# Hyena's short convolution: past tokens into the middle product, coming tokens into an array preloaded with the bias, joined later by VectorE

## The chip, the cores and the metric

The kernel runs on one core of one Trainium2 chip. The metric is device time in microseconds (us), from the start to the end of one execution; several runs are taken and their median counts. Beside these runs one execution was recorded by the hardware profiler; its trace gives every instruction's start and duration. Five engines work side by side, each through its own instruction stream in a fixed order: TensorE (PE in the profile; PEld is its weight load), VectorE (DVE), ScalarE (ACT), GpSimd (POOL) and SyncE (SP). In this kernel SP and POOL, and ACT for a few constants, issue the DMA transfers.

## The reference

One encoder layer on 256 tokens of width 2048, all in float32. A wide projection of the input feeds two branches, a chunked gated linear attention (GLA) and an order-2 Hyena; sigmoid gates mix the two, one output projection, a layer norm, a squared-ReLU MLP and a second layer norm follow. The change touches the Hyena branch alone:

```python
def _short_conv(u, w, b):                 # 3 taps along the tokens, per channel
    y = lax.conv_general_dilated(u, w[:, None, :], (1,), [(1, 1)], ...)
    return y + b
...
uc = _short_conv(u, conv_w, conv_b)
v, x1, x2 = jnp.split(uc, 3, axis=-1)
z = v
for o, gate in enumerate((x1, x2)):
    zf = jnp.fft.rfft(z, n=2 * L, axis=1)
    zc = jnp.fft.irfft(zf * filt_f[None, :, o], n=2 * L, axis=1)[:, :L]
    z = gate * (zc + skip[o] * z)
```

So each token's value is tap 0 times the token before it, plus tap 1 times itself, plus tap 2 times the token after it, plus a bias.

## The kernel before

**Stages.** The opening and the q, k, r projections with the Hyena filters (lines 251 to 505); v and the first gate with the GLA (511 to 691); the Hyena stage (694 to 827); the second gate's projection `g2` (841 to 845); the two branches' output projections and the merge; `w_out` and layer norm; the MLP. Weights come in blocks of 128 x 2048 (1 MB). Every float32 product is made of three: `split_hi_lo` (83) has ACT cast a block half to `whi` and DVE subtract to get `wlo`, and PE multiplies high by high, high by low and low by high.

**Weight stream.** `fetch` (92) issues the load of the block two ahead of the one in use, on SP, and its two splits. There are three raw buffers and three each of half-blocks `whi` and `wlo`, so a split of a half-block waits until PE has finished with the half-block three before it.

**A token group** (`token_group`, 208) makes one 256 x 512 piece of a projection: 4 blocks, 96 matmuls (lines 204 to 206), into two of the four banks of the PSUM pool `mmp`, one for each half of the tokens. After each block it calls `pump` (117), which counts a clock on by one and runs what `later(d, fn)` (113) has put off until then, in the order of due time and then of entry. So `later(3, ...)` entered at a group's end is run behind the third block of the next group.

**Order.** The program is traced in that order; a planner then fixes each engine's order. It takes, of the instructions whose inputs are there by its own estimate, the one traced first. `tc.keep_in_program_order` pins an instruction behind the one traced before it on its engine. On the chip every engine keeps the planned order and waits where an input is late, with all that stands behind it.

**Buffers.** A pool's tag with one buffer is used by one tile after the other: the first write of the next tile waits until the last instruction that uses the tile before is done, wherever that was traced. `qp` and `hp` have one buffer per tag. Tag `G` of `qp` (16 KB in a partition) holds `g_sb` (495), then `conv_sb` (699), then `g2_sb` (841).

**Hyena stage.** Four rounds `s`, each with the token groups `uv`, `ux`, `ux` (for v, x1, x2; 512 channels each) and a group `go` of the GLA's output projection. At the end of the first three stands `short_conv` (706). It makes three products of the group's PSUM banks with tap rows on DVE: `past` (tap 0), `y` (tap 1, the tile `cv` or `cx` in the profile) and `ahead` (tap 2), each in two halves (line 710, six instructions). It adds the bias to `y` (711). Then four POOL DMAs (718) add `past`, one partition on, and `ahead`, one partition back, into `y`, each with a 2 KB one for the row that goes over from one half of the tokens to the other. The `ahead` pair writes what the `past` pair wrote, so it waits for it to land. `conv_sb` has the tap rows and the bias row (1 MB, loaded anew for each group, line 704), `past` and `ahead`.

Behind each `uv` group 4 Hyena steps `j` are entered (2 chunks of 256 channels times 2 orders): `hy_load` (`Tl`, the filter's spectrum), `hy_fwd` (transform, 6 matmuls), `hy_mul` (DVE: `Z`, `pa`, `pb`, then the split `Yh`, `Yl`) and `hy_inv` (6 matmuls `yp`, the gate product `zf`, and for the second order a transpose `yT` of `zf` and its store `yo`, `yd`). Step j's `hy_fwd` and `hy_mul` are due 7 + 4j blocks behind the `uv` group and its `hy_inv` 11 + 4j, each time behind a third block. The last round's steps run on into the `g2` groups; the inverse of its last step is due behind the third block of the third of them.

Of the kernel before, what the change touches and what calls it, by code (L numbers as in the profile page):

```python
# [9 lines left out]
F32 = mybir.dt.float32  # L10
F32R = mybir.dt.float32r
I32 = mybir.dt.int32
AF = mybir.ActivationFunctionType
ALU = mybir.AluOpType
DRAM = bass.MemoryType.DRAM

P = 128
D = 2048
L = 256
NT = L // P  # L20
# [7 lines left out]
CW = D // NCH  # L28
# [14 lines left out]
def block_kernel(  # L43
# [24 lines left out]
    nc = tc.nc  # L68
    MM = nc.tensor.matmul

    base = ctx.enter_context(tc.tile_pool(name="base", bufs=1))
# [3 lines left out]
    drp = ctx.enter_context(tc.tile_pool(name="drp", bufs=1, space=DRAM))  # L75
# [4 lines left out]
    def psum_side(name):  # L80
        return sdp.tile([P, 512], F32, tag="sd", name=name)

    def split_hi_lo(hi, lo, src):
        return (nc.scalar.copy(hi, src),  # L84
                nc.vector.tensor_tensor(lo, src, hi.bitcast(F32), op=ALU.subtract))  # L85
# [20 lines left out]
    def weight_half(n, h):  # L106
        return (wp.tile([P, D // 2], F32R, tag="whi", bufs=3, name=f"whi{n}_{h}"),
                wp.tile([P, D // 2], F32R, tag="wlo", bufs=3, name=f"wlo{n}_{h}"))
# [4 lines left out]
    def later(d, fn):  # L113
        clock[1] += 1
        side.append((clock[0] + d, clock[1], fn))
# [92 lines left out]
    def token_group(act, name):  # L208
        pss = [psum_main(f"{name}_{tb}") for tb in range(NT)]
        for b in range(4):  # L210
            token_products(pss, act, [next_block()], range(NT), b)
            pump()
        return pss
# [34 lines left out]
    qp = qkg.enter_context(tc.tile_pool(name="qp", bufs=1))  # L248
# [5 lines left out]
    with tc.tile_pool(name="xp", bufs=1) as xp, tc.tile_pool(name="xq", bufs=1) as xq:  # L254
# [25 lines left out]
        for i in range(3):  # L280
            t = weight_half(-1, i)
# [52 lines left out]
    def mm3(ps, lh, ll, rh, rl, start, stop, hold=False):  # L334
        ins = MM(ps, lh, rl, start=start, stop=False)
        if hold:
            tc.keep_in_program_order(ins)
        MM(ps, lh, rh, start=False, stop=False)
        MM(ps, ll, rh, start=False, stop=stop)
# [130 lines left out]
    for i in range(2 * NCH):  # L470
        c, o = divmod(i, 2)
# [223 lines left out]
    hp = hstk.enter_context(tc.tile_pool(name="hp", bufs=1))  # L695
    cst = {}
    yh_dram = {}

    conv_sb = qp.tile([P, 4, 2 * 512], F32, tag="G", name="conv_sb")
    taps = conv_sb[:, 0:2].rearrange("p a b -> p (a b)").rearrange("p (a b) -> p a b", a=4)  # L700
    past, ahead = (conv_sb[:, 2 + i].rearrange("p (t d) -> p t d", t=NT) for i in range(2))

    def load_taps(i):
        nc.sync.dma_start(conv_sb[:, 0:2].rearrange("p a b -> p (a b)"), conv_rows[i:i + 1, :].broadcast_to([P, 2048]))

    def short_conv(pss, i, tag, name):
        y = hp.tile([P, NT, 512], F32, tag=tag, name=name)
        for j, dst in ((0, past), (1, y), (2, ahead)):
            for tb in range(NT):
                nc.vector.tensor_tensor(dst[:, tb], pss[tb], taps[:, j], op=ALU.mult)  # L710
        nc.vector.tensor_tensor(y, y, taps[:, 3:4].broadcast_to([P, NT, 512]), op=ALU.add)
        for dst, src in (
            (y[1:P], past[0:P - 1]),
            (y[0:1, 1], past[P - 1:P, 0]),
            (y[0:P - 1], ahead[1:P]),
            (y[P - 1:P, 0], ahead[0:1, 1]),
        ):
            nc.gpsimd.dma_start(dst, src, accum_op=ALU.add)
        if i + 1 < 12:
            later(2, lambda: load_taps(i + 1))  # L720
        return y

    def hy_v(s):
        def run():
            z = tuple(hp.tile([P, NT, 512], F32R, tag=t, name=f"{t}{s}") for t in ("vh", "vl"))
            split_hi_lo(z[0], z[1], cst.pop(("v", s)))
            for i in range(2):
                cst[("z", 2 * s + i, 0)] = tuple(t[:, :, i * CW:(i + 1) * CW] for t in z)
        return run

    def gate_part(n, c):
        return cst[(n, c // 2)][:, :, c % 2 * CW:(c % 2 + 1) * CW]

    def hy_load(c, o):
        def run():
            t = hp.tile([P, 2, 3, CW], F32, tag="Tl", name=f"Tl{c}{o}")
            nc.gpsimd.dma_start(t, T_dram[(c, o)])
            cst[("T", c, o)] = t
        return run

    def hy_fwd(c, o):
        def run():
            t = cst.pop(("T", c, o))
            zh, zl = cst.pop(("z", c, o))
            z = hp.tile([P, 3, 2, CW], F32, tag="Z", name=f"Z{c}{o}")
            for ri in range(2):
                pz = psum_side(f"Zp{c}{o}{ri}")
                mm3(pz.rearrange("p (a b) -> p a b", a=2), dfth[:, ri], dftl[:, ri], zh, zl, True, True, hold=True)
                nc.scalar.copy(z[:, 2:0:-1, ri, :], pz.rearrange("p (a b) -> p a b", a=2))
            cst[("Z", c, o)] = (t, z)  # L750
        return run

    def hy_mul(c, o):
        def run():
            t, z = cst.pop(("Z", c, o))
            a = hp.tile([P, 3, 2, CW], F32, tag="pa", name=f"pa{c}{o}")
            b = hp.tile([P, 3, 2, CW], F32, tag="pb", name=f"pb{c}{o}")
            TT = nc.vector.tensor_tensor
            full = [P, 3, 2, CW]
            TT(z[:, 0], z[:, 1], z[:, 2], op=ALU.add)  # L760
            TT(a, z, t[:, 0, :, None, :].broadcast_to(full), op=ALU.mult)
            TT(b, z[:, :, ::-1, :], t[:, 1, :, None, :].broadcast_to(full), op=ALU.mult)
            TT(a[:, :, 0], a[:, :, 0], b[:, :, 0], op=ALU.subtract)
            TT(a[:, :, 1], a[:, :, 1], b[:, :, 1], op=ALU.add)
            y = a[:, 1:3]
            TT(y, y, a[:, 0:1].broadcast_to([P, 2, 2, CW]), op=ALU.add)
            yh = hp.tile([P, 2, 2, CW], F32R, tag="pb", name=f"Yh{c}{o}")
            yl = hp.tile([P, 2, 2, CW], F32R, tag="Yl", name=f"Yl{c}{o}")
            split_hi_lo(yh, yl, y)
            cst[("Y", c, o)] = (yh, yl)  # L770
        return run

    def hy_inv(c, o):
        def run():
            yh, yl = cst.pop(("Y", c, o))
            py = psum_side(f"yp{c}{o}")
            py3 = py.rearrange("p (a b) -> p a b", a=2)
            mm3(py3, dfth[:, 2], dftl[:, 2], yh[:, :, 0], yl[:, :, 0], True, False)
            mm3(py3, dfth[:, 3], dftl[:, 3], yh[:, :, 1], yl[:, :, 1], False, True)
            zf = hp.tile([P, NT, CW], F32, tag="zf", name=f"zf{c}{o}")  # L780
            nc.vector.tensor_tensor(zf, py3, gate_part(("x1", "x2")[o], c), op=ALU.mult)
            if o == 0:
                z = tuple(hp.tile([P, NT, CW], F32R, tag=t, name=f"{t}{c}") for t in ("zh", "zl"))
                split_hi_lo(z[0], z[1], zf)
                cst[("z", c, 1)] = z
            else:
                pt = psum_side(f"yT{c}")
                for cc in range(2):
                    for tb in range(NT):
                        nc.tensor.transpose(pt[:, cc * L + tb * P:cc * L + (tb + 1) * P], zf[:, tb, cc * P:(cc + 1) * P], ident)  # L790
                pt = pt.rearrange("p (a b) -> p a b", a=2)
                if c >= NCH - 2:
                    split_hi_lo(yhT[:, 2 * c:2 * c + 2, 0], yhT[:, 2 * c:2 * c + 2, 1], pt)
                    return
                yo = hp.tile([P, 2, L], F32, tag="zf", name=f"yo{c}")
                nc.scalar.copy(yo, pt)
                yd = drp.tile([P, 2, L], F32, tag=f"yd{c}", name=f"yd{c}")
                nc.gpsimd.dma_start(yd, yo)
                yh_dram[c] = yd
        return run  # L800

    go_done = [0]
# [7 lines left out]
            nc.vector.tensor_tensor(mg[:, tb], mg[:, tb], pss[tb], op=ALU.mult)  # L810

    load_taps(0)
    for s in range(NCH // 2):
        for k, n in enumerate(("v", "x1", "x2")):
            pss = token_group(xT, f"u{n}{s}")
            cst[(n, s)] = short_conv(pss, 3 * s + k, n, f"c{n}{s}")
            if k == 0:
                later(5, hy_v(s))
                steps = [(2 * s + j % 2, j // 2, 4 * j) for j in range(4)]
                for c, o, d in steps:  # L820
                    later(6 + d, hy_load(c, o))
                    later(7 + d, hy_fwd(c, o))
                for c, o, d in steps:
                    later(11 + d, hy_inv(c, o))
                for c, o, d in steps:
                    later(7 + d, hy_mul(c, o))
        gla_o_group()
# [276 lines left out]
    with tc.high_priority(), tc.issue_after(done.ins):  # L1104
# [3 lines left out]
        y, ym, t, v, rs, nb = (ep.tile([P, 1], F32, tag=f"fin{i}", name=f"fin{i}") for i in range(6))  # L1108
# [150 lines left out]
```

## Time and profile before

| | us |
|---|---|
| median of 3 runs (1874.43 to 1877.8) | 1877.04 |
| the profiled execution, whole | 1882.77 |
| its span, first to last instruction | 1881.0 |
| DVE busy (share of the span) | 1284.3 (68%) |
| ACT busy | 891.3 (47%) |
| POOL busy | 69.3 (4%) |

The mean granted TensorE clock is 0.994 of full speed. DMA moved 399.43 MB. All points in time below are us from the start of the span. In the views, `out<-in` names tiles, `x` counts instructions, the value in square brackets is the engine's idle time just before the instruction and what ended it, and PEclk is the share of full speed that the clock throttle granted to PE. A line of the windows view has, behind the stretch and its length, each engine's busy time with its count of instructions, then PEclk, the DMA engines' busy share and GB/s. The round s = 0 of the Hyena stage begins at about 460 us, and the `g2` groups at about 885 us.

### The profile page before, as it was taken

How to read it: one execution, taken by the hardware profiler on the slowest of the kernel's cores; microseconds unless marked ns; L12 is line 12 of the kernel's file. 1: busy time of each engine (PE TensorE's matmuls, PEld its weight loads, DVE VectorE, ACT ScalarE, POOL GpSimd, SP SyncE). 2: the span in 40 equal slices, each digit the busy share in tenths (PEclk: the TensorE clock that was granted, in tenths of full speed). 3: DMA queues.
4: the chain of work that ended last, by engine and by line, in shares of the span. 5: the costliest groups of instructions: out<-in, count | busy, mean ns of one | idle time of the engine just before them, and what ended most of it. 6: DMA issues, size and time to landing. Idle time of an engine off the chain costs nothing.

```text
span 1881.0 us, 22915 instructions
## 1 busy us (share of the span) xinstructions
PE 1846.8 (98%) x8999; PEld 1549.6 (82%) x8999; DVE 1284.3 (68%) x1578; ACT 891.3 (47%) x1160; POOL 69.3 (4%) x104
## 2 busy tenths in 40 slices
PE   9999999999899899899999999999999999999999
PEld 7878888888778787777888889888888888888887
DVE  6879878765578887898845557666555555565567
ACT  6545558665334444344544446444434443443332
POOL 0000000000010101011000000000000000000000
PEclk9999999999999999999999999999999999999999
DMA  8657664436696869778555564555555555555553
GB/s 320 216 208 289 241 241 169 168 138 219 201 276 234 261 210 288 239 240 254 216 183 198 227 250 175 198 214 183 197 185 197 190 191 195 188 197 183 201 182 132
DMA packets 65117, 399.43 MB, mean 212 GB/s; under 512 B 8009, under 2 KB 10457, under 8 KB 24305
## 3 DMA queue, kind: packets, MB, share of 16 engines
q1 hardware_dynamic: 47808, 336.61, 49.8%
q0 software_dynamic: 10144, 41.55, 8.4%
q10 hardware_dynamic: 7056, 19.80, 2.9%
q8 instruction: 71, 1.16, 0.3%
q14 instruction: 38, 0.30, 0.0%
HBM read 369.15 MB, written 16.25 MB: 205 GB/s over the span
## 4 chain that ended last, share of the span: by engine, by line
PE 77%; DMA 8%; DVE 7%; issue 6%; ACT 1%; POOL 0%; SPq 0%; DVEq 0%; ACTq 0%; POOLq 0%
PE f L145 12%; PE f L149 6%; PE w L206 6%; PE w L204 6%; PE w L205 6%; DMA cx<-conv_sb 3%; DMA cv<-conv_sb 3%; PE g L205 3%; PE g L206 3%; PE g L204 3%; DVE wlo L85 2%; PE ho L206 2%; PE ho L205 2%; PE ho L204 2%; PE v L204 1%
## 5 line engine op out<-in xcount | busy, mean ns | idle before, releaser
L85 DVE TENSOR_TENSOR wlo<-raw,whi 128x1024 fp32r<-128x1024 f32 x584 | 711.0, 1221 | 398.0 <-ACT whi L84 396.1
L84 ACT CAST whi<-raw 128x1024 fp32r<-128x1024 f32 x584 | 613.3, 1052 | 633.0 <-PE w L206 188.3
L145 PE MATMUL f<-hT,whi 128*128 128x512 f32 x984 | 235.1, 391 | 0.0
L145 PEld LDWEIGHTS f<-hT,whi 128*128 128x128 f32 x984 | 180.8, 188 | 35.0
L205 PE MATMUL w<-wlo,f 128*128 128x512 f32 x480 | 186.7, 389 | 0.0
L206 PE MATMUL w<-whi,f 128*128 128x512 f32 x480 | 186.7, 389 | 0.0
L204 PE MATMUL w<-whi,f 128*128 128x512 f32 x480 | 167.4, 389 | 0.0
L149 PEld LDWEIGHTS f<-hT,wlo 128*128 128x128 f32 x984 | 126.2, 191 | 4.8
L149 PE MATMUL f<-hT,wlo 128*128 128x256 f32 x984 | 127.7, 283 | 0.0
L205 PE MATMUL ux<-wlo,xT 128*128 128x512 f32 x256 | 101.8, 398 | 7.6 <-DVE wlo L85 7.6
L206 PEld LDWEIGHTS w<-whi,f 128*128 128x128 f32 x480 | 90.1, 188 | 18.8
L205 PEld LDWEIGHTS w<-wlo,f 128*128 128x128 f32 x480 | 90.1, 188 | 18.7
L204 PEld LDWEIGHTS w<-whi,f 128*128 128x128 f32 x480 | 90.1, 188 | 18.6
L157 ACT ACTIVATE f_l<-f 128x256 f32<-128x256 f32 x64 | 24.6, 384 | 162.3 <-PE f L145 159.4
L205 PE MATMUL g<-wlo,xT 128*128 128x512 f32 x256 | 100.2, 391 | 0.6 <-DVE wlo L85 0.6
L206 PE MATMUL ux<-whi,xT 128*128 128x512 f32 x256 | 100.8, 394 | 0.0
L206 PE MATMUL g<-whi,xT 128*128 128x512 f32 x256 | 99.7, 390 | 0.0
L158 DVE SCALAR_TENSOR_TENSOR f_s<-f,f_l 128x256 f32<-128x256 f32 x64 | 27.2, 425 | 105.2 <-ACT f_l L157 105.2
L204 PE MATMUL ux<-whi,xT 128*128 128x512 f32 x256 | 93.3, 394 | 2.5 <-ACT whi L84 2.5
L204 PE MATMUL g<-whi,xT 128*128 128x512 f32 x256 | 93.0, 391 | 0.0
L205 PEld LDWEIGHTS ux<-wlo,xT 128*128 128x128 f32 x256 | 48.7, 190 | 21.7 <-DVE wlo L85 11.8
L205 PE MATMUL go<-wlo,yg 128*128 128x512 f32 x128 | 53.0, 414 | 13.7 <-DVE wlo L85 13.7
(430 smaller groups left out, 3212.1 us busy)
## 6 DMA issues: line engine op xcount, KB each, us to landing
raw<-wblk SPq DMA_DIRECT2D x300, 1024.0 KB, 4.8
Td<-T POOLq DMA_DIRECT2D x16, 768.0 KB, 4.7
conv_sb<-conv_rows SPq DMA_DIRECT2D x12, 1024.0 KB, 8.8
Tl<-Td POOLq DMA_DIRECT2D x16, 768.0 KB, 5.7
w<-w4s ACTq DMA_DIRECT2D x16, 512.0 KB, 5.4
cx<-conv_sb POOLq DMA_DIRECT2D x16, 508.0 KB, 9.2
xw<-first SPq DMA_DIRECT2D x5, 896.0 KB, 12.9
zr<-ln_rows ACTq DMA_DIRECT2D x4, 1024.0 KB, 9.4
```

The source lines that it names most:

```text
L84: return (nc.scalar.copy(hi, src), nc.vector.tensor_tensor(lo, src, hi.bitcast(F32), op=ALU.subtract))
L85: nc.vector.tensor_tensor(lo, src, hi.bitcast(F32), op=ALU.subtract))
L145: MM(ps[:, :, ts], hi[:, js], act[:, kt, :, ts], start=(kt == 0 and opens), stop=(kt == KT - 1))
L149: MM(ps[:, 0, ts], lo[:, js], act[:, kt, 0, ts], start=False, stop=False)
L157: nc.scalar.activation(low, ps[:, 1], AF.Copy, scale=scale)
L158: nc.vector.scalar_tensor_tensor(dst, ps[:, 0], scale, low, op0=ALU.mult, op1=ALU.add)
L204: MM(pss[tb], sh, wh, start=(kt == 0), stop=False)
L205: MM(pss[tb], sh, wl, start=False, stop=False)
L206: MM(pss[tb], sl, wh, start=False, stop=(kt == KT - 1))
```

## The change

`short_conv` no longer adds the bias on DVE before the DMAs. The bias row is left out of the tap load (768 KB instead of 1 MB) and goes by two DMAs of 256 KB on SP into a new tile `rest`; the `past` pair adds into `y` and the `ahead` pair into `rest`, so neither waits for the other. A new DVE instruction, `finish`, adds `rest` to `y`; it is run three blocks later and pinned in program order. `rest` is one tile, so the bias of the next group (`more`, also three blocks later, behind `finish`) is loaded when `finish` has read it. The tap load is due one block earlier, and the split of v (`hy_v`) too.

To make room for `rest` (4 KB), two tiles of `hp` are given up: `zf` and `yo` become row 7 of `conv_sb`, and `zh` moves to tag `sum` of the pool `base`. The store `yd<-yo` is issued one block later.

```diff
-    conv_sb = qp.tile([P, 4, 2 * 512], F32, tag="G", name="conv_sb")
-    taps = conv_sb[:, 0:2].rearrange("p a b -> p (a b)").rearrange("p (a b) -> p a b", a=4)
-    past, ahead = (conv_sb[:, 2 + i].rearrange("p (t d) -> p t d", t=NT) for i in range(2))
+    conv_sb = qp.tile([P, 8, 512], F32, tag="G", name="conv_sb")
+    taps = conv_sb[:, 0:3]
+    past, ahead = conv_sb[:, 3:5], conv_sb[:, 5:7]
+    rest = hp.tile([P, NT, 512], F32, tag="rest", name="rest")
 
     def load_taps(i):
-        nc.sync.dma_start(conv_sb[:, 0:2].rearrange("p a b -> p (a b)"), conv_rows[i:i + 1, :].broadcast_to([P, 2048]))
+        nc.sync.dma_start(taps.rearrange("p a b -> p (a b)"), conv_rows[i:i + 1, 0:1536].broadcast_to([P, 1536]))
+
+    def load_bias(i):
+        for tb in range(NT):
+            nc.sync.dma_start(rest[:, tb], conv_rows[i:i + 1, 1536:2048].broadcast_to([P, 512]))
...
-        nc.vector.tensor_tensor(y, y, taps[:, 3:4].broadcast_to([P, NT, 512]), op=ALU.add)
         for dst, src in (
             (y[1:P], past[0:P - 1]),
             (y[0:1, 1], past[P - 1:P, 0]),
-            (y[0:P - 1], ahead[1:P]),
-            (y[P - 1:P, 0], ahead[0:1, 1]),
+            (rest[0:P - 1], ahead[1:P]),
+            (rest[P - 1:P, 0], ahead[0:1, 1]),
         ):
             nc.gpsimd.dma_start(dst, src, accum_op=ALU.add)
+
+        def finish():
+            tc.keep_in_program_order(nc.vector.tensor_tensor(y, y, rest, op=ALU.add))
+
+        def more():
+            if i + 1 < 12:
+                load_bias(i + 1)
+
         if i + 1 < 12:
-            later(2, lambda: load_taps(i + 1))
+            later(1, lambda: load_taps(i + 1))
+        later(3, finish)
+        later(3, more)
         return y
...
-            zf = hp.tile([P, NT, CW], F32, tag="zf", name=f"zf{c}{o}")
+            zf = conv_sb[:, 7].rearrange("p (t d) -> p t d", t=NT)
...
-                z = tuple(hp.tile([P, NT, CW], F32R, tag=t, name=f"{t}{c}") for t in ("zh", "zl"))
+                z = (base.tile([P, NT, CW], F32R, tag="sum", name=f"zh{c}"),
+                     hp.tile([P, NT, CW], F32R, tag="zl", name=f"zl{c}"))
...
-                yo = hp.tile([P, 2, L], F32, tag="zf", name=f"yo{c}")
+                yo = conv_sb[:, 7].rearrange("p (a l) -> p a l", a=2)
                 nc.scalar.copy(yo, pt)
-                yd = drp.tile([P, 2, L], F32, tag=f"yd{c}", name=f"yd{c}")
-                nc.gpsimd.dma_start(yd, yo)
-                yh_dram[c] = yd
+
+                def keep():
+                    yd = drp.tile([P, 2, L], F32, tag=f"yd{c}", name=f"yd{c}")
+                    nc.gpsimd.dma_start(yd, yo)
+                    yh_dram[c] = yd
+                later(1, keep)
...
     load_taps(0)
+    load_bias(0)
...
-                later(5, hy_v(s))
+                later(4, hy_v(s))
```

## The prediction

> **What bounds the kernel now.** I read the page's chain first, then the Hyena stage boundary by boundary in the windows view, then DVE's timeline where PE stands idle, and last the DMAs. The chain that ended last:
>
> ```profile
> PE 77%; DMA 8%; DVE 7%; issue 6%; ACT 1%; POOL 0%; SPq 0%; DVEq 0%; ACTq 0%; POOLq 0%
> ```
>
> PE carries it; most of the 8% of DMA is the accumulating DMAs of the Hyena stage. The windows around the ends of the token groups (stretch, length, busy PE, PEld, DVE, ACT, POOL, PEclk, DMA share, GB/s):
>
> ```profile
> 505.00:521.00 16.00, 10.98 (x37) 8.31 (x36) 9.15 (x12) 4.93 (x5) 1.65 (x2) 0.79 0.57 163
> 521.00:547.00 26.00, 24.63 (x110) 20.06 (x109) 21.20 (x22) 10.35 (x11) 3.26 (x5) 1.00 0.88 258
> 585.00:600.00 15.00, 13.92 (x61) 11.19 (x61) 15.00 (x18) 6.32 (x6) 1.98 (x3) 1.00 0.63 209
> 611.00:626.00 15.00, 14.34 (x64) 11.14 (x63) 14.76 (x17) 7.63 (x8) 2.46 (x4) 1.00 0.82 246
> 640.00:660.00 20.00, 15.82 (x60) 12.52 (x59) 15.88 (x17) 6.31 (x6) 2.29 (x3) 0.83 0.83 246
> 750.00:770.00 20.00, 15.26 (x58) 12.10 (x57) 15.28 (x16) 5.92 (x6) 2.29 (x3) 0.83 0.79 221
> 858.00:878.00 20.00, 16.55 (x67) 13.20 (x66) 16.11 (x16) 6.99 (x7) 3.92 (x5) 0.91 0.82 206
> 885.00:960.00 75.00, 75.00 (x335) 61.79 (x334) 58.69 (x59) 38.92 (x47) 3.25 (x6) 1.00 0.59 210
> 648.00:652.00 4.00, 3.57 (x8) 2.81 (x9) 4.00 (x5) 0.00 (x0) 0.00 (x0) 0.50 0.35 97
> ```
>
> PE's idle time is a window's length less its busy time; what a lower clock costs I estimate as busy time times (1 - PEclk). At the end of x1's group PE loses 5.02 + 2.3 us in round 0 (505:521), but 0.66 us in round 1 (611:626). At the end of x2's it loses 1.37 us in round 0 (521:547), and 4.18 + 2.7, 4.74 + 2.6 and 3.45 + 1.5 us in the next three (640:660, 750:770, 858:878). At v's it is 1.08 us at full clock (585:600). So only idle of some 3 us and more brings the clock down, and the `g2` stage (885:960) loses nothing: 335 matmuls in 75 us, 0.224 us each, or 21.5 us for a group's 96. The reasons stand in DVE's timeline, where the square brackets name what DVE waited for:
>
> ```profile
> 502.29 2.36 DVE L85 TENSOR_TENSOR wlo<-raw,whi 128x1024 fp32r<-128x1024 f32 x2 [4.10 <-ACT whi L84]
> 509.83 0.69 DVE L710 TENSOR_TENSOR conv_sb<-ux,conv_sb 128x512 f32<-128x512 f32 x1 [3.98 <-DMA cv<-conv_sb]
> 640.59 1.75 DVE L762 TENSOR_TENSOR pb<-Z,Tl 128x1536 f32<-128x1536 f32 x1
> 644.76 1.29 DVE L710 TENSOR_TENSOR conv_sb<-ux,conv_sb 128x512 f32<-128x512 f32 x2 [2.42 <-DMA cx<-conv_sb]
> 753.81 1.29 DVE L710 TENSOR_TENSOR conv_sb<-ux,conv_sb 128x512 f32<-128x512 f32 x2 [2.98 <-DMA cx<-conv_sb]
> 862.38 1.29 DVE L710 TENSOR_TENSOR conv_sb<-ux,conv_sb 128x512 f32<-128x512 f32 x2 [1.69 <-DMA cx<-conv_sb]
> ```
>
> The next group's products wait for the DMAs that still read `past` and `ahead`; behind them in DVE's order stand the `wlo` splits that PE needs.
>
> **The DMAs side by side.** Before, they go one pair after the other (chain view):
>
> ```profile
> 488.03 12.71 DMA cv<-conv_sb
> 501.56 8.25 DMA cv<-conv_sb
> 623.04 11.22 DMA cx<-conv_sb
> 635.18 9.56 DMA cx<-conv_sb
> ```
>
> The engines are shared meanwhile: from 488 to 501 the accumulating queue has a quarter of their time, the weights' queue most of the rest.
>
> ```profile
> q1 hardware_dynamic: 438, 3.24, 70.2%
> q0 software_dynamic: 176, 0.52, 24.9%
> ```
>
> A pair's own work is thus 0.249 x 13 = 3.2 us of all engines. Side by side, the second pair lies behind the first on one queue: at best it lands 3.2 us behind it, at 12.7 + 3.2 = 15.9 us, at worst after both durations, 21.0. I take 18, about the middle, since the weights go on beside it. The Trainium skill speaks against the change here: "SBUF — State Buffer", section "Can I just issue two DMAs to hit both halves?", has two concurrent DMAs only 6% above a single one. By that, (12.71 + 8.25) / 1.06 = 19.8 us, an estimate, and round 0 below would keep some 1 us more; no row here shows two such DMAs at once.
>
> The issue is earlier as well, since it no longer stands behind the bias addition:
>
> ```profile
> 481.79 0.68 DVE L710 TENSOR_TENSOR conv_sb<-uv,conv_sb 128x512 f32<-128x512 f32 x1
> 484.78 0.68 DVE L710 TENSOR_TENSOR conv_sb<-uv,conv_sb 128x512 f32<-128x512 f32 x1
> 486.51 1.22 DVE L711 TENSOR_TENSOR cv<-cv,conv_sb 128x1024 f32<-128x1024 f32 x1
> ```
>
> The products end at 485.5, so the pair of v's first group lands at 503.5 (501.4 to 506.5) instead of 509.8. `finish` stands there behind the splits that end at 504.65, so it waits nothing at my value and 1.9 us at worst. Twelve additions of 1.22 us are removed and twelve of the same shape put in: DVE's load stays. But here `finish` comes ahead of the six products, not behind them as line 711 does: I charge 0.5 us of PE idle. Round 0 gains 7.3 - 0.5 = **6.8 us**. Its x2 boundary waited for no DMA for long (1.37 us at full clock), so I leave it.
>
> **Where `finish` stands later, and the bias.** From x1's group on, a Hyena step's `hy_mul` is due behind the same third block and was entered earlier, so `finish` is pinned behind its last DVE instruction, `Yl`:
>
> ```profile
> 619.26 1.22 DVE L85 TENSOR_TENSOR vl<-cv,vh 128x1024 fp32r<-128x1024 f32 x1
> 621.53 1.22 DVE L711 TENSOR_TENSOR cx<-cx,conv_sb 128x1024 f32<-128x1024 f32 x1
> 623.80 1.21 DVE L85 TENSOR_TENSOR Yl<-pa,Yh 128x1024 fp32r<-128x1024 f32 x1
> ```
>
> By then v's DMAs are in (18 us are less than a group's 21.5), so DVE does not stand there. But x1's bias can be loaded only then, and POOL holds x1's `ahead` pair until it is in. Line 711 and `vl` leave the place ahead of `Yl`: it ends at 625.0 - 2.4 = 622.6, `finish` at 623.8. For the bias I go by these rows, page and stage view:
>
> ```profile
> conv_sb<-conv_rows SPq DMA_DIRECT2D x12, 1024.0 KB, 8.8
> yr<-yd POOLq DMA_DIRECT2D x6, 256.0 KB, 4.7
> q1 hardware_dynamic: 47808, 336.61, 49.8%
> ```
>
> Two loads of 256 KB take between 4.7 and 8.8 us; I take 6, nearer the smaller. The `ahead` pair, issued at 630, takes 8.25 to 9.56 (above): 639, with ends of 635 (both shorter, some overlap) and 645 (`Yl` no earlier: 626.2 + 8.8 + 9.6). It is needed when `pb` ends at 642.34. So the waits of 2.42, 2.98 and 1.69 us go, and with 1.8 us of idle left, where DVE is merely full, the clock should stay up as in the 1.08 us windows: 2.42 + 2.7 + 2.98 + 2.6 + 1.69 + 1.5 = **13.9 us**. At x1's ends line 711 and `vl` no longer stand ahead of a split: some 0.35 us three times, **1.1 us**.
>
> What I cost at nothing: the DMA work grows by 0.25 MB a group, at 0.498 x 1881 / 336.61 = 2.8 us per MB 0.7 us, hidden while raw blocks are loaded ahead; if not, 12 x 0.7 = 8 us are the end. On SP the bias waits for `finish` ahead of raw loads, but the planner puts loads that are ready sooner first. The earlier tap load frees SP from waiting for line 711. On POOL `Tl` and `yd` stand behind a held `ahead` pair at worst; both are needed a group later. `hy_v` follows `finish` by a block, and ACT no longer waits there for the DMA. The two moved tiles keep single buffers.
>
> **What row 7 costs.** `conv_sb` is now used as long as any `zf` is, and `g2_sb` is the next tile of tag `G`. That such a hand-over is a real wait shows one tile earlier: the last reader of `g_sb` ends at 424.69, and the first load of `conv_sb` starts 0.08 us later.
>
> ```profile
> 423.94 0.75 DVE L646 SCALAR_TENSOR_TENSOR y<-o,rs,g_sb 128x512 f32<-128x512 f32 x1
> 424.77 0.33 SPq L704 DMA_DIRECT2D conv_sb<-conv_rows  x1
> ```
>
> So the first write of `g2_sb`, the sigmoid of the first `g2` group, must wait for the transposes of the last `zf` (round 3, step 3), which before came two groups later. Until then the first two `g2` groups hold all four banks, and the third can't start. The rows around the end of the second group:
>
> ```profile
> 933.86 0.60 ACT L845 ACTIVATE g_sb<-g 128x512 f32<-128x512 f32 x1 [0.98 <-PE g L206]
> 940.03 1.21 DVE L85 TENSOR_TENSOR Yl<-pa,Yh 128x1024 fp32r<-128x1024 f32 x1
> L335 PE MATMUL yp<-Yl,dfth x2: 389/389/389, 946.2 to 946.8; 128*128 128x512 f32 x2
> L790 PE MATMUL yT<-ident,zf x4: 270/272/272, 953.2 to 953.5; 128*128 128x128 f32 x4
> L781 DVE TENSOR_TENSOR zf<-yp,cx x1: 683/683/683, 948.1 to 948.1; 128x512 f32<-128x512 f32 x1
> ```
>
> The sigmoid at 933.86 waited for the group's first bank; the second is full three matmuls later, so PE runs dry at 934.5. `Yl` ends at 941.24; six `yp` matmuls at half clock (3.57 us for 8 in window 648:652, so 0.446 each) take 2.7 us, `zf` 0.68, the transposes with their waits an estimated 0.6, the sigmoid 0.60: PE goes on at 945.8. Of these 11.3 us, 1.7 (six matmuls at 0.224, 0.3 of transposes) leave the third group, and the clock takes 2.4 us behind it, as 2.3 to 2.7 above: **-12 us**. Ends: 8 us (`Yl` earlier by one of the splits ahead of it, no clock loss) and 16 us (a further split and a weight load in the way).
>
> **Sum.** 6.8 + 13.9 + 1.1 - 12.0 = 9.8 us less. The profiled execution's span goes from 1881.0 to 1871.2 and its time from 1882.77 to 1873.0. It stands 5.7 us above the median of the runs, 1877.04, which becomes 1867.2. A difference of 0.2%, 3.75 us, is about what can be told from no change.
>
> **Rivals.**
>
> *The bias comes too late (ends slower).* POOL holds x1's `ahead` pair for a bias that waits for `finish`, which waits its turn behind `Yl`. If the pair lands at 644.8 or later instead of 639, the x2 boundaries wait as before and the 13.9 us are not gained: 12.0 - 6.8 - 1.1 = 4.1 us slower, 1881.1; each us later costs three more. For it speaks the end of 645; against it, that this needs all three durations at their longest.
>
> *Row 7 holds nothing back.* If the hand-over of tag `G` goes by what is overwritten and not by the tile, the first sigmoids go ahead, and the 12 us are not paid: 1877.04 - 21.8 = 1855.2. Against it: the load at 424.77 writes the first half of the tile, and the reader that it waited for reads the last eighth.
>
> *A half gain.* The pair in round 0 lands at the worst (1.9 us and its clock loss remain, some 4 us), and the bias is late in one or two rounds of three (some 5 us each): the gain shrinks from 21.8 to about 12, and the 12 us eat it: 1877. For it speaks that the four rows of the chain vary by 1.5 us within a kind, which is half the slack of 3 us.
>
> **How the numbers follow.** The forecast 0.52, with a range of its own from 1861 to 1873 (the ends of the row 7 cost); the late bias 0.25; the half gain 0.17; row 7 without a wait 0.06. Faster 0.52 + 0.06 = 0.58, same 0.17, slower 0.25. The range reaches from 1858, which leaves out the 0.06 and a little of the forecast's lower tail, to 1884, where the late bias with 16 us for row 7 still lies within 1 us or so.
>
> **What the profile will show.** All four accumulating DMAs of a group issued within some 3 us, the second pair landed some 18 us behind the first issue; no window at round 0's x1 boundary with a clock of 0.8; DVE's product at the x2 boundaries without a wait for `cx<-conv_sb`; `finish` right behind `Yl`; and in the second half of the `g2` stage, which now has none, idle PE of about 10 us before the third group, the first two sigmoids both behind the last `yT`. The prediction is wrong if the `ahead` pair lands later than `pb` ends, if raw loads land late because SP stands at the bias, or if `g2` shows no idle.

## The result, and the profile after

The changed kernel takes 1897.0 us (median of 4 runs, 1893.5 to 1898.2) where the kernel before takes 1877.4 us beside it: a ratio of 1.0101, with a 95% interval of 1.008 to 1.0123. It is **1.0% slower**; the prediction was 1867 us, faster, in a range up to 1884. The profiled execution took 1898.19 us with a span of 1896.4 us, against 1882.77 and 1881.0.

The page's chain of the changed kernel, and three pieces of its chain view (start, length, what). DVE's share has risen from 7% to 10% and that of DMA has fallen from 8% to 6%, and a weight block (`raw`) now stands in the chain with its whole 12.8 us:

```profile
PE 76%; DVE 10%; DMA 6%; issue 6%; ACT 1%; POOL 0%; SPq 0%; DVEq 0%; POOLq 0%; ACTq 0%
...
587.11 12.82 DMA raw<-wblk
600.03 1.06 ACT whi L84
...
620.56 6.90 DMA rest<-conv_rows
```

The windows at the ends of the token groups of the changed kernel (columns as before):

```profile
501.00:517.00 16.00, 15.80 (x70) 12.77 (x69) 12.87 (x15) 7.21 (x7) 3.27 (x4) 1.00 0.83 256
520.00:546.00 26.00, 23.01 (x102) 18.70 (x101) 22.10 (x22) 11.08 (x12) 2.42 (x4) 1.00 0.79 259
605.00:622.00 17.00, 12.93 (x49) 9.87 (x48) 16.29 (x18) 5.07 (x6) 2.88 (x4) 0.90 0.79 243
640.00:660.00 20.00, 16.62 (x67) 13.21 (x66) 17.30 (x18) 7.29 (x8) 2.28 (x3) 0.91 0.77 252
717.00:735.00 18.00, 14.08 (x61) 10.95 (x60) 18.00 (x19) 7.04 (x8) 2.88 (x4) 1.00 0.81 248
753.00:772.00 19.00, 14.34 (x54) 11.71 (x55) 16.08 (x17) 5.68 (x7) 2.29 (x3) 0.82 0.67 232
828.00:846.00 18.00, 13.55 (x53) 10.13 (x52) 18.00 (x21) 6.55 (x7) 2.88 (x4) 0.91 0.67 200
866.00:886.00 20.00, 16.89 (x67) 13.47 (x67) 17.36 (x18) 7.19 (x8) 2.87 (x4) 0.91 0.71 194
936.00:957.00 21.00, 13.10 (x55) 9.95 (x54) 10.75 (x11) 6.19 (x9) 0.00 (x0) 0.84 0.14 51
```

The windows of the kernel before that answer to 717:735 and 828:846:

```profile
717.00:735.00 18.00, 17.24 (x77) 13.58 (x76) 17.70 (x20) 8.70 (x9) 4.47 (x6) 1.00 0.85 253
828.00:846.00 18.00, 17.61 (x78) 13.94 (x77) 17.22 (x19) 8.79 (x9) 3.45 (x5) 1.00 0.87 251
```

By idle time and clock, counted as in the prediction, the change in loss is, in us:

| place | before | after | gain |
|---|---|---|---|
| x1's end, round 0 (501:517 after) | 7.3 | 0.2 | +7.1 |
| x2's end, round 0 (520:546) | 1.4 | 3.0 | -1.6 |
| x1's ends, rounds 1 to 3 (605:622, 717:735, 828:846) | 1.8 | 15.0 | -13.2 |
| x2's ends, rounds 1 to 3 (640:660, 753:772, 866:886) | 19.1 | 18.2 | +0.9 |
| `g2` stage (936:957) | 0 | 10.0 | -10.0 |

For 753:772 the idle time is the 6.1 us of the waits view below, since the window begins inside it. The sum is 16.8 us lost. The span grew by 15.4; the profiled execution had been 2.0 us ahead before the Hyena stage began, which the change doesn't touch, so 17.4 us were lost from there on.

What is new stands at the ends of x1's groups. DVE's timeline of the changed kernel:

```profile
499.79 2.36 DVE L85 TENSOR_TENSOR wlo<-raw,whi 128x1024 fp32r<-128x1024 f32 x2 [3.62 <-ACT whi L84]
601.12 1.23 DVE L85 TENSOR_TENSOR wlo<-raw,whi 128x1024 fp32r<-128x1024 f32 x1 [5.90 <-ACT whi L84]
602.26 0.69 DVE L774 TENSOR_TENSOR Z<-Z 128x512 f32<-128x512 f32 x1
613.25 1.22 DVE L85 TENSOR_TENSOR wlo<-raw,whi 128x1024 fp32r<-128x1024 f32 x1
618.92 1.23 DVE L725 TENSOR_TENSOR cv<-cv,rest 128x1024 f32<-128x1024 f32 x1
635.54 0.68 DVE L715 TENSOR_TENSOR cx<-ux,conv_sb 128x512 f32<-128x512 f32 x1
637.78 0.69 DVE L715 TENSOR_TENSOR conv_sb<-ux,conv_sb 128x512 f32<-128x512 f32 x1 [1.56 <-DMA rest<-conv_sb]
640.05 1.75 DVE L776 TENSOR_TENSOR pb<-Z,Tl 128x1536 f32<-128x1536 f32 x1
750.65 0.69 DVE L715 TENSOR_TENSOR conv_sb<-ux,conv_sb 128x512 f32<-128x512 f32 x1 [4.23 <-DMA rest<-conv_sb]
863.21 0.69 DVE L715 TENSOR_TENSOR conv_sb<-ux,conv_sb 128x512 f32<-128x512 f32 x1 [1.27 <-DMA rest<-conv_sb]
```

At 601.12 DVE has stood 5.90 us for ACT, which waited for the block that landed at 599.93. Behind that split come, in DVE's fixed order, the Hyena step (`Z` to `pb`), the six products and the split at 613.25 that PE needs: PE then stands 3.4 us. The same block (issued 9.4 us into x1's group in both kernels), in the DMA view of the kernel before and of the changed one:

```profile
raw<-wblk SPq DMA_DIRECT2D x1, 1024.0 KB, 5.2
```

```profile
raw<-wblk SPq DMA_DIRECT2D x1, 1024.0 KB, 12.8
cv<-conv_sb POOLq DMA_DIRECT2D x1, 508.0 KB, 9.1
rest<-conv_sb POOLq DMA_DIRECT2D x1, 508.0 KB, 13.0
```

It goes out 3.4 us behind v's first accumulating DMA (583.67) and lands 1.5 us behind the last one (598.40). In the kernel before it had gone out at 594.90, ahead of v's first accumulating DMA (596.58). In the waits view of the Hyena stage and the first `g2` groups (455:965; who waited for what: us in total, times, longest), first the kernel before, then the changed one:

```profile
PE go L205 <- DVE wlo L85: 13.7, 4, 4.7
PE ux L205 <- DVE wlo L85: 7.6, 9, 2.5
ACT whi L84 <- DMA raw<-wblk: 4.3, 1, 4.3
```

```profile
PE go L205 <- DVE wlo L85: 15.5, 4, 6.1
PE ux L205 <- DVE wlo L85: 15.5, 10, 3.4
ACT whi L84 <- DMA raw<-wblk: 27.5, 6, 6.6
DVE conv_sb L715 <- DMA rest<-conv_sb: 7.1, 3, 4.2
```

### The profile page after: what moved, and what is told of

Read it like the earlier page. It is cut to its first block, busy times and chain, and to the rows that moved or that the text cites. A ratio compares the mean times of both kernels' runs of the same rounds, so it can differ in the third digit from the quotient of the medians.

```text
span 1896.4 us, 22995 instructions
## 1 busy us (share of the span) xinstructions
PE 1848.9 (97%) x8999; PEld 1551.0 (82%) x8999; DVE 1284.0 (68%) x1578; ACT 893.5 (47%) x1160; POOL 69.3 (4%) x104
## 4 chain that ended last, share of the span: by engine, by line
PE 76%; DVE 10%; DMA 6%; issue 6%; ACT 1%; POOL 0%; SPq 0%; DVEq 0%; POOLq 0%; ACTq 0%
PE f L145 12%; PE f L149 6%; PE w L204 6%; PE w L205 6%; PE w L206 6%; DMA raw<-wblk 3%; PE g L205 3%; PE g L206 3%; PE g L204 3%; DVE wlo L85 2%; DMA rest<-conv_sb 2%; PE ho L205 2%; PE ho L206 2%; PE ho L204 2%; PE v L204 1%
## 6 DMA issues: line engine op xcount, KB each, us to landing
rest<-conv_sb POOLq DMA_DIRECT2D x12, 508.0 KB, 10.1
```

## The experiments

The theory after the result has three parts: (A) two pairs of accumulations at once make weight blocks late, and PE stands at x1's ends; (B) row 7 costs 10 us in `g2`; (C) at x2's ends DVE waits for a pair that POOL held for the bias. Ratios are to the kernel before, run beside each on the same chip; the chips differ, so ratios are compared, not medians. e3_no_bias, e4_no_v_ahead and g2_plain_early leave out a part of the sum and are probes alone.

| run | median, us | ratio (95%) |
|---|---|---|
| the change | 1897.0 | 1.0101 (1.0080 to 1.0123) |
| e1_row7 | 1886.8 | 1.0054 (1.0039 to 1.0069) |
| e2_v_later1 | 1897.7 | 1.0114 (1.0095 to 1.0132) |
| e3_no_bias | 1894.9 | 1.0099 (1.0071 to 1.0127) |
| e5_finish2 | 1897.6 | 1.0114 (1.0095 to 1.0132) |
| e4_no_v_ahead | 1880.9 | 1.0024 (1.0005 to 1.0042) |
| f2_serial | 1884.9 | 1.0031 (1.0016 to 1.0047) |
| g1_serial_keep | 1873.0 | 0.9976 (0.9956 to 0.9996) |
| f3_plain | 1868.1 | 0.9949 (0.9933 to 0.9965) |
| f4_plain_serial | 1868.6 | 0.9949 (0.9933 to 0.9966) |
| g2_plain_early | 1874.6 | 0.9985 (0.9968 to 1.0003) |
| g3_plain_fin2 | 1883.1 | 1.0030 (1.0017 to 1.0043) |
| h1_v_between | 1861.8 | 0.9910 (0.9882 to 0.9938) |

### Row 7 (B)

```diff
+            if o == 1 and c >= NCH - 2:
+                zf = hp.tile([P, NT, CW], F32, tag="x1", name=f"zf{c}{o}")
+            else:
+                zf = conv_sb[:, 7].rearrange("p (t d) -> p t d", t=NT)
-            zf = conv_sb[:, 7].rearrange("p (t d) -> p t d", t=NT)
```

> The changed kernel, but the last two zf tiles (chunks 6 and 7, second step) lie in the dead tile x1 and not in row 7 of conv_sb, so that conv_sb has no reader left when the g2 stage begins. Theory (row 7 holds the hand-over of tag G): the idle time of 6.42, 0.79 and 0.69 us ahead of the third g2 group goes, and the half clock behind it, some 2.5 us: about 1887 us instead of 1897. Rival (the sigmoids are late for another reason, such as ACT's order): 1897, idle time as it is.

Measured: 1886.8 us, 0.47% of the 1.01% back, or 8.8 us. In the changed kernel, ACT's and PE's timelines show the wait; below them the same window with row 7 free:

```profile
950.94 2.07 ACT L864 ACTIVATE g_sb<-g 128x512 f32<-128x512 f32 x4 [5.72 <-PE yT L805]
946.53 0.80 PE L335 MATMUL yp<-Yl,dfth 128*128 128x512 f32 x1 [6.42 <-DVE Yl L85]
950.25 0.66 PE L805 MATMUL yT<-ident,conv_sb 128*128 128x128 f32 x4 [0.79 <-DVE conv_sb L795]
951.59 0.50 PE L204 MATMUL g<-whi,xT 128*128 128x512 f32 x1 [0.69 <-ACT g_sb L864]
```

```profile
936.00:957.00 21.00, 21.00 (x96) 17.36 (x95) 14.69 (x14) 10.00 (x12) 0.00 (x0) 1.00 0.42 150
```

All four sigmoids stand behind the last `yT`; freed, PE runs the whole 21 us at full clock. B holds.

### The pairs side by side (A)

Two attempts to part the pairs, e2_v_later1 and f2_serial, did not part them. e2_v_later1:

```diff
+        later(1, coming) if i % 3 == 0 else coming()    # coming(): the two DMAs into rest
```

> The changed kernel, but in v's groups alone the pair of DMAs of the coming tokens is issued one block (some 6 us) later than the pair of the past ones, not at its side. Theory (1 MB of accumulation in one burst takes the DMA engines from the weight blocks, which land 12 to 13 us after their issue instead of 5, and DVE's Hyena step stands behind those blocks' splits): the blocks land in under 9 us again, and of the PE idle time at the ends of x1's groups of rounds 1 to 3 (3.45, 3.40, 3.42 us with 0.4 to 0.6 ahead of it, and a lower clock) most goes: 1884 to 1888 us instead of 1897. Round 0 may give back 1 to 2 us, since its pair lands later. Rival (those stalls come from the order in which the splits, the products and the Hyena step stand on DVE): the stalls stay within 0.5 us, 1896 to 1899.

Measured: 1897.7 us and unchanged stalls, but the pair went out as before: it is only traced later, and nothing held POOL. This run says nothing about A. e4_no_v_ahead takes the pair away:

```diff
-        ):
+        )[:2 if i % 3 == 0 else 4]:
             nc.gpsimd.dma_start(dst, src, accum_op=ALU.add)
```

> The changed kernel without the two DMAs of the coming tokens in v's groups (their part of v is left out of the sum); those of x1 and x2 stay. Issued one block later they still went out at once, 587.04 beside 585.95, since nothing held POOL, so this takes them away. Theory (the burst of two pairs takes the DMA engines from the weight blocks): the block issued 9.4 us into x1's group of round 1 lands within 8 us and not 12.8, and the idle time of 3.4 us at the ends of x1's groups of rounds 1 to 3 goes with its low clock: 1884 to 1888 us instead of 1897. Rival (one pair, issued earlier in the group than before the change, is enough to make the block late): idle time of 2.5 us or more stays there, 1893 to 1897.

Measured: 1880.9 us, by the ratios 14.5 us less than the change, where 9 to 13 were expected. The block lands in 7.9 us, and x1's end runs through at full clock (DMA view and windows; the last row is a later x2 end, for below):

```profile
raw<-wblk SPq DMA_DIRECT2D x1, 1024.0 KB, 7.9
```

```profile
605.00:622.00 17.00, 17.00 (x75) 13.74 (x74) 16.40 (x18) 8.03 (x9) 2.29 (x3) 1.00 1.00 288
845.00:865.00 20.00, 17.81 (x71) 14.53 (x72) 17.31 (x18) 6.52 (x8) 3.15 (x5) 0.91 0.72 226
```

Rounds 2 and 3 have no stall at x1's end either. That the second pair causes the stalls is shown; whether its being beside the other does, or only its amount, is for the serial runs. f2_serial puts a small DMA that reads v's sum between the pairs, and frees row 7; g1_serial_keep also pins the order:

```diff
...
+            keep = tc.keep_in_program_order if i in (3, 6, 9) else (lambda ins: ins)
+            if k == 2 and i in (3, 6, 9):
+                keep(nc.gpsimd.dma_start(drp.tile([2, 512], F32, tag="sy", name=f"sy{i}"), y[0:2, 1]))
-            nc.gpsimd.dma_start(dst, src, accum_op=ALU.add)
+            keep(nc.gpsimd.dma_start(dst, src, accum_op=ALU.add))
```

> The changed kernel with row 7 freed as in the run e1_row7 (1887 us), and in v's groups of rounds 1 to 3 the coming pair held on POOL until the past pair has landed (a DMA of 4 KB that reads its sum stands between), as the two pairs were before the change. Theory (side by side is what makes the weight blocks late): the stalls of 3.4 us at the ends of x1's groups go, 1873 to 1878 us. Rival (the time of issue and not the neighbourhood of the pairs): the stalls stay, 1885 to 1888. If the weight blocks only become late at another place, something between.

> As f2_serial (row 7 freed, base 1887 us; in v's groups of rounds 1 to 3 the coming pair behind the past pair), but with the order on POOL kept as written: in f2_serial the coming pair had gone out ahead of the small DMA that was to hold it (591.67, the small one 600.17). Theory (a burst of two pairs makes the weight blocks late): the block issued 9.4 us into x1's group of round 1 lands within 9 us and not 12.6, and of the stalls of 3.4 us at the ends of x1's groups of rounds 1 to 3 at least half goes: 1872 to 1880 us. Rival (the amount accumulated by the end of x1's group decides, side by side or not): the stalls move by a few us and stay, 1884 to 1888.

In f2_serial the planner let the coming pair go ahead of the small DMA, so the pairs still lay side by side; the stalls of 3.4 us stayed, and it tells no more than e1_row7. In g1_serial_keep (DMA view of the block, the past pair and the coming pair; windows):

```profile
raw<-wblk SPq DMA_DIRECT2D x1, 1024.0 KB, 7.7
...
cv<-conv_sb POOLq DMA_DIRECT2D x1, 508.0 KB, 8.4
...
rest<-conv_sb POOLq DMA_DIRECT2D x1, 508.0 KB, 8.1
```

```profile
605.00:622.00 17.00, 17.00 (x77) 13.74 (x77) 16.85 (x20) 8.82 (x9) 2.89 (x4) 1.00 0.91 279
```

The block lands in 7.7 us and not 12.8, and x1's ends have no idle time in any of the three rounds. The ratio falls from e1_row7's 1.0054 to 0.9976, 0.8% or 15 us; from that of f2_serial, which differs by the pinned order alone, it falls by 0.55%, or 10 us (1.0031; its x2's ends had lost less than e1_row7's). The same bytes go through the same queue, one pair behind the other: for this block A is the neighbourhood in time, not the amount. That two pairs are always needed is not shown: in the kernel before, a block issued 0.9 us behind v's first pair of round 0 (488.89) took 12.2 us beside that pair alone.

### The bias and x2's ends (C)

```diff
 def more():                                  # e3_no_bias
-    if i + 1 < 12:
-        load_bias(i + 1)
+    return
 ...
-later(3, finish)                             # e5_finish2
-later(3, more)
+later(2, finish)
+later(2, more)
```

> The changed kernel without the bias loads of groups 2 to 12 (their bias is left out of the sum; rest keeps what it had). POOL then holds the coming pair only for finish. Theory (at the ends of x2's groups DVE's product waits for a pair that POOL held for the bias): the pair of x1's group lands some 6 us earlier, about 631 instead of 637.75, DVE's waits of 1.56, 4.23 and 1.27 us at line 715 go, and the low clock there with them: 8 to 13 us less, 1884 to 1889. Rival (DVE is full there and the order decides, the wait only fills a gap): at most 2 us less, 1895 to 1897.

> The changed kernel with the joining addition and the bias load behind it due one block earlier (two blocks after the group and not three), which puts the addition ahead of the six Hyena products on DVE and not behind Yl. Theory (the place behind Yl is what makes the bias, and so x1's coming pair, late): the bias of x1's group lands some 12 us earlier, POOL holds nothing, the x2 boundaries lose their waits for the pair (7.1 us together) and part of their low clock: 8 to 12 us less, 1885 to 1889. Rival (DVE now stands at the addition until the pair of 15.6 us has landed, with splits behind it): the waits move to line 725, 1895 to 1905.

Without the bias loads no wait of DVE for the pair is left, and x2's ends of rounds 1 to 3 keep 1.74 us of idle time at full clock:

```profile
644.00:664.00 20.00, 18.27 (x81) 14.78 (x80) 17.61 (x18) 7.82 (x9) 3.92 (x5) 1.00 0.79 244
```

So C is right about the wait. But the whole time hardly moved: by the ratios 0.4 us, less than the runs scatter, where 8 to 13 were expected; it came out as the rival had it, though the wait did not merely fill a gap. In the profiled executions the stretch from the start of the Hyena stage to that of `g2` took 427.3 us, 4.9 less than in the change. Of the 13 us won at x2's ends some 6 can be seen to go elsewhere: 4.6 at x2's end in round 0, which had three stalls of 0.8, 2.0 and 3.5 us and a low clock instead of one stall of 3.0, and 1.5 at x1's end in round 2, where a stall of 3.4 us as before now brought the clock down. So what C alone is worth in the whole time is not shown. e5_finish2 cleared x2's ends as well (20.00 busy of 20 at full clock in 640:660), but paid chiefly at x1's, with two stalls of 1.8 to 3.4 us in each of the three rounds, since the addition now stands ahead of splits and waits for the pairs (waits view):

```profile
DVE cx L725 <- DMA rest<-conv_sb: 17.3, 6, 4.6
DVE cv L725 <- DMA raw<-wblk: 8.0, 2, 4.1
DVE cv L725 <- DMA rest<-conv_sb: 7.1, 2, 3.7
```

The rival held for e5_finish2: the waits moved to line 725, and 1897.6 us lies in its range.

### Versions that use what was found

f3_plain: the bias comes with the taps again and DVE adds it behind the products; the coming tokens are copied into `rest`, so there is no bias to wait for; row 7 is not used. f4_plain_serial adds f2_serial's small DMA, which again held nothing back. g2_plain_early is f3_plain without the added bias, so that the pairs go out together. g3_plain_fin2 and h1_v_between move the joining addition of v's groups:

```diff
+        nc.vector.tensor_tensor(y, y, taps[:, 3:4].broadcast_to([P, NT, 512]), op=ALU.add)   # not in g2_plain_early
...
-            nc.gpsimd.dma_start(dst, src, accum_op=ALU.add)        # for rest
+        nc.gpsimd.dma_start(rest[0:P - 1], ahead[1:P])
+        nc.gpsimd.dma_start(rest[P - 1:P, 0], ahead[0:1, 1])
...
-        later(3, finish)
+        later(2 if i % 3 == 0 else 3, finish)                      # g3_plain_fin2
+        later(2.5 if i % 3 == 0 else 3, finish)                    # h1_v_between
```

> Side by side, but without the bias in the array: the coming tokens are copied, not accumulated, into rest (its last row is zeroed once), the bias comes with the taps again and VectorE adds it behind the products, as before the change; row 7 is no longer used (zf lies in Yl's buffer, yo in zl's). It costs twelve more VectorE additions of 1.22 us, and POOL has no bias to wait for. Theory: the 10 us of row 7 and the waits for x1's coming pair at the ends of x2's groups (7.1 us and clock) go; the stalls at the ends of x1's groups stay, since both pairs are still one burst, unless a copy takes less of the engines than an accumulation: 1878 to 1883 us with them, 1868 to 1873 without. Rival (DVE is what bounds the boundaries): the added work eats the gain, 1885 or more.

> As f3_plain, and in v's groups of rounds 1 to 3 the copy waits on POOL until the past pair has landed. Theory: this has round 0's gain of the change (5.8 us) and none of its three losses; the stalls at the ends of x1's groups are as before the change, 1865 to 1871 us, faster than both kernels. Rival (the twelve more additions, or the copy landing late at x1's ends, are in the way): 1875 or more.

> As f3_plain (1868 us), without the addition of the bias behind the products (the bias is left out of the sum), so that the past pair goes out as early as the copy, at its side. It tells whether the stalls at x1's ends went in f3_plain because a copy is short (4.4 us where the accumulating pair took 13) or because the past pair went out 4.8 us later. Theory (the copy is short): no stall over 1 us at x1's ends of rounds 1 to 3; with twelve additions less 1860 to 1867 us. Rival (the time of issue): stalls of 2 us or more are back there, 1870 or more.

> As f3_plain (1868 us), with the joining addition of v's groups one block earlier, so that x1's copy, which overwrites what that addition reads, can go out as soon as x1's products are there. Theory (the three waits of 7.6 us together at the ends of x2's groups come from the copy that waits for the addition behind Yl): these waits go and with them part of the idle time of 3.25, 4.46 and 2.53 us and the clock of 0.9 there: 1858 to 1865 us. Rival (VectorE is full there): idle time of 2.4 us or more stays at each, as in e4_no_v_ahead, which had no such waits: 1866 to 1869; or the addition now waits for v's past pair, 1870 or more.

> As f3_plain (1868 us), with the joining addition of v's groups half a block earlier than there and half a block later than in g3_plain_fin2: on VectorE it stands behind pb and two additions ahead of x1's six products, when v's past pair has landed some 8 us before. Theory (the waits at the ends of x2's groups come from x1's copy, which waits for the addition behind Yl and then goes out behind x1's past pair): the copy goes out with the products, ahead of the past pair, and lands within 6 us, the three waits of 7.6 us together go, and with them the idle time at the ends of x2's groups, as in g3_plain_fin2, which has none there: 1855 to 1864 us. Rival (the idle time at x2's ends comes back as idle time at x1's ends, where VectorE has 1.22 us more ahead of a split): 1866 or more.

f3_plain and f4_plain_serial: 1868 us both, 0.5% faster than the kernel before, at the better end of what was expected. The copy of v, issued 4.8 us ahead of the past pair because the bias addition stands between, takes 4.4 us; the block then takes 9.1 us, and x1's end has no stall. g2_plain_early decides why. Its copy lies beside the past pair, and the copy and the block take:

```profile
rest<-conv_sb POOLq DMA_DIRECT2D x1, 508.0 KB, 14.4
...
raw<-wblk SPq DMA_DIRECT2D x1, 1024.0 KB, 11.4
```

Stalls of 2.3 to 3.4 us are back at x1's ends, and with twelve additions less it takes 1874.6 us. So the rival held: the time of issue, not copy against accumulation. At x2's ends f3_plain keeps three waits of 7.6 us: x1's copy waits for `cv`'s joining addition and goes out behind x1's past pair, in 13.9 us. g3_plain_fin2 ended them, but its addition stood 19.4 us in all for v's past pair (waits view), and the stalls came back at x1's ends; 1883 us. h1_v_between puts the addition where v's pair is in and x1's products have not begun. Its windows at x1's and x2's ends of rounds 1 and 2, and x1's copy:

```profile
605.00:622.00 17.00, 15.49 (x67) 12.18 (x66) 14.42 (x15) 6.19 (x7) 2.72 (x4) 1.00 0.79 243
630.00:650.00 20.00, 18.33 (x81) 14.83 (x81) 19.96 (x21) 8.24 (x9) 3.31 (x5) 1.00 0.74 230
708.00:725.00 17.00, 15.49 (x67) 12.18 (x66) 15.79 (x18) 6.22 (x6) 2.71 (x4) 1.00 0.79 247
735.00:755.00 20.00, 18.33 (x82) 14.83 (x81) 20.00 (x22) 8.21 (x10) 3.33 (x5) 1.00 0.76 234
```

```profile
rest<-conv_sb POOLq DMA_DIRECT2D x1, 508.0 KB, 4.4
```

1861.8 us, 0.9% (0.6 to 1.2%) faster than the kernel before and the fastest run of this study. Two stalls of 1.1 and 0.4 us come back at each of x1's ends and 1.7 us stays at x2's, where none was expected, all at full clock. g3_plain_fin2's expectation says that e4_no_v_ahead had no waits for the pair at x2's ends; it had 2.5 us of them in three.

## Why the prediction was wrong, step by step

- **Round 0, 6.8 us: right.** The last of the four DMAs lands 16.1 us after the first issue (the second pair goes out 1.6 us later and takes 14.5) and not 18; `finish` at 502.07 waits for nothing, and x1's end gains 7.1 us. "I leave it", of x2's end there, missed 1.6 us: a block issued at 510.31 beside x1's pairs took 10.1 us, and DVE stood 3.11 us for it at 521.54 with a Hyena step behind.
- **"What I cost at nothing": the first step that failed, 14.3 us off.** It had the added bytes hidden "while raw blocks are loaded ahead", and among its ends only a price per MB, 8 us. The price was the burst: the block issued within it took 12.8 us where it had taken 5.2, and a Hyena step on DVE stood behind its split. The prediction had measured that the engines are shared with the weights' queue, and used it for how long the pairs take, never for how long a block beside them takes. Its own first DVE line showed that price: the 4.10 us at 502.29 are ACT's wait for the block of 488.89, which took 12.2 us beside one pair. Round 0 of the changed kernel gave the same late block (12.9 us) no chance to hurt, since no Hyena step stands there in DVE's order; in rounds 1 to 3 one does. The 1.1 us forecast for x1's ends became a loss of 13.2. The sign "raw loads land late because SP stands at the bias" came, but not for that cause: the block went out on time, 9.4 us into the group.
- **x2's ends, 13.9 us: 0.9 came; the second step that failed, 13.0 us off.** In round 1 the pair landed at 637.75 against 639 forecast; in round 2 it came 2.7 us later within its round. What failed is when it is needed: "when `pb` ends at 642.34" took DVE's order over from the kernel before. The planner put the first product of `ahead` in front of `pa` and `pb`, so DVE wanted it behind the product of 635.54 and stood until 637.78. So the loss of the rival "the bias comes too late" happened with the pair on time. The 1.8 us of idle at full clock that the step left is what e3_no_bias has (1.74) and h1_v_between (1.67).
- **Row 7, 12 us: right in mechanism, 10.0 by the windows, and 8.8 us by the run that freed it.** The named signs are there: 7.9 us of idle PE where about 10 were named, and the sigmoids behind the last `yT`.
- **The sum.** -9.8 us became about +16.8: 14.3 from the blocks at x1's ends, 13.0 from x2's, 1.3 from round 0, less 2.0 on row 7. In the rival of the half gain, "about 12" holds for a bias late in one round; late in two, by its own terms, it leaves 7.8 us.

By the Trainium skill, "SBUF — State Buffer", section "Can I just issue two DMAs to hit both halves?", the pairs would have taken 19.8 us, an estimate. In series they took 18.6 us in g1_serial_keep (the last of the four goes out 10.3 us after the first and takes 8.3), side by side 14.7 in the same group of the changed kernel: a quarter longer in series, where the rule has 6%. But the 3.9 us that the pairs gain side by side cost the block beside them 5.1 us, 12.8 against 7.7. A rule that was not weighed bears on the first failed step: the Trainium skill, "DMA: Bandwidth & Descriptors", section "Issuing engines are not separate DMA queues", has transfers of all issuing engines interleave on the same DMA engines. The block on SP's queue agrees with it: it takes 5.2 us ahead of POOL's pair, 7.7 behind the start of one and 12.8 behind that of two.

## What to carry to other kernels

Price a DMA burst by what lands beside it: find the load that is issued within it, give it the burst's landing time, and follow who waits for that load in each engine's fixed order, in every round and not in the first alone. When an edit moves or removes instructions under a planner, its order round a boundary has to be taken as new; a slack computed from the old order is no slack. To part two transfers, give the second something real to wait for and keep it in order; tracing it later parted nothing here.

## What the runs showed that was not expected

A copy of 508 KB took 4.4 us ahead of an accumulating pair and 13.9 to 14.4 us when it was issued 1.1 to 3.4 us behind one, so its place in the queue makes it more than three times as long.

The clock did not follow the length of one stall. In the changed kernel stalls of 3.4 us at x1's ends left PEclk at 0.90 and 0.91 in two rounds and at 1.00 in the one between (717:735), while in e4_no_v_ahead a stall of 2.4 us at an x2 end (2.2 us of it inside the window 845:865) had 0.91, and one of 2.6 us in another round 1.00. So a single stall of 2.4 to 3.4 us cost up to 1.6 us of clock (17.81 busy at 0.91) or nothing, and the forecast's line of 3 us was too sharp. The Trainium skill, "TensorE: Matmul & The Clock Gate", section "Why this matters for your kernels", warns of idle gaps above some 3 us, and its section "What's actually happening" says that activity is judged in a window of some 3.4 us that runs freely; that would let equal stalls differ by where they fall, as they do here, but no run was made to show it, and the stall of 2.4 us lies below its figure.
